# Closing a row-mean kernel: the last store awaited behind the barriers, and the last piece scaled and summed by one accumulating instruction

## The chip, the cores and the metric

The kernel runs on one core of a Trainium2 chip. Its time is the device time of one execution in microseconds; the kernel before takes 162.94 us (median of 4 runs, 162.81 to 163.14). "The span" is what the profile shows: from the first to the last instruction of the program, 161.5 us. The difference is the runtime's own work around the program.

## The reference

```python
batch, seq, dim = 32, 512, 1024
x: float32 [32, 512, 1024]; divisor = 1024.0

def reference(x, divisor):
    return (np.sum(x, axis=-1) / divisor).astype(np.float32)
```

67.1 MB are read and 64 KB written, so the kernel lives from the stream of loads.

## The kernel before

SyncE issues all loads. 16,384 rows lie as 128 partitions of 128 rows; 120 of each go into the output tile `res` in large loads, the last eight into `fin` through ever smaller ones, so that little work is left when the last bytes arrive. The last row of each partition comes in three pieces: `pa` (448 elements, summed by ScalarE), `pb` (256, summed by VectorE) and `pc` (320, with two more columns that take those two sums). `q` collects VectorE's sums; `r` is zero but for one column, where ScalarE puts its share of a row, already scaled. So `fin` is `q` times the scale plus `r`. The end, with cuts:

```python
# ... main loads and sums into res; two small loads into q ...
act_sum(r[:, j : j + 1], row[:, c:], by=scale)                     # ScalarE, 256 elements
nc.vector.reduce_sum(out=q[:, j : j + 1], in_=row[:, :c], axis=AX) # VectorE, 768 elements
# ... loads of pa, pb, pc; res scaled on GpSimd and stored ...
act_sum(pc[:, D - b : D - b + 1], pa)
nc.vector.reduce_sum(out=pc[:, D - b + 1 :], in_=pb, axis=AX)
nc.vector.reduce_sum(out=q[:, L - 1 :], in_=pc, axis=AX)
nc.vector.scalar_tensor_tensor(out=fin, in0=q, scalar=scale, in1=r, op0=MULT, op1=ADD)
tc.keep_in_program_order(nc.sync.dma_start(out=o_last, in_=fin))
```

After this the framework closes the program: SyncE waits for everything that is still under way, the last store included; then come two rounds of a barrier of all engines, between which GpSimd clears the program's semaphores.

Of the kernel before, what the change touches and what calls it, by code (L numbers as in the profile page):

```python
# [1 line left out]

# [4 lines left out]

F32 = mybir.dt.float32
ADD = mybir.AluOpType.add
MULT = mybir.AluOpType.mult  # L10
COPY = mybir.ActivationFunctionType.Copy
AX = mybir.AxisListType.X


def start_loads_at_once(nc):



    sp = mybir.EngineType.SP
    first, body = nc.main_func.blocks[0], nc.main_func.blocks[1]  # L20
    loads = []
    for i in body.instructions:
        if i.engine == sp:
            if type(i).__name__ != "InstDMACopy" or (i.sync_info and i.sync_info.on_wait):
                break
            loads.append(i)
    names = {i.name for i in loads}
    assert names
    body.instructions = [i for i in body.instructions if i.name not in names]
    at = next(  # L30
        k for k, i in enumerate(first.instructions) if i.engine == sp and type(i).__name__ == "InstDrain"
    )
    first.instructions = first.instructions[:at] + loads + first.instructions[at:]


@with_exitstack
def kernel(
    ctx: ExitStack,
    tc: tile.TileContext,
    x: bass.AP,  # L40
    divisor: float,
    out: bass.AP,
):
    nc = tc.nc
    nc.at_finalize(start_loads_at_once)
    xf = x.flatten_outer_dims()
    N, D = xf.shape
    P = nc.NUM_PARTITIONS
    scale = 1.0 / float(divisor)
    J = N // P  # L50
    assert J * P == N


    L = 8
    M = J - L
    x_main = bass.AP(tensor=x.tensor, offset=0, ap=[[M * D, P], [D, M], [1, D]])
    x_last = bass.AP(tensor=x.tensor, offset=P * M * D, ap=[[L * D, P], [D, L], [1, D]])
    o_main = bass.AP(tensor=out.tensor, offset=0, ap=[[M, P], [1, M]])
    o_last = bass.AP(tensor=out.tensor, offset=P * M, ap=[[L, P], [1, L]])


    main = [(14, 0)] * 6 + [(14, 4), (14, 6), (8, 4)]
    last = [(4, 2), (2, 1)]
    assert sum(n for n, _ in main) == M and sum(n for n, _ in last) == L - 2
    bulk = ctx.enter_context(tc.tile_pool(name="bulk", bufs=3))
    one = ctx.enter_context(tc.tile_pool(name="one", bufs=1))
    psum = ctx.enter_context(tc.tile_pool(name="junk", bufs=4, space=bass.MemoryType.PSUM))

    res = one.tile([P, M], F32, name="res")
    fin = one.tile([P, L], F32, name="fin")  # L70
    q = one.tile([P, L], F32, name="q")
    r = one.tile([P, L], F32, name="r")
    nc.gpsimd.memset(r, 0.0)  # L73

    def load(dst, src):
        tc.keep_in_program_order(nc.sync.dma_start(out=dst, in_=src))  # L76

    def act_sum(dst, src, by=1.0):
        n = src.shape[-1]
        junk = psum.tile([P, D], F32, name="junk")  # L80
        nc.scalar.activation(junk[:, :n], src, COPY, scale=by, accum_out=dst)  # L81

    def sums(dst, t, rows, on_act):
        d = rows - on_act
        for i in range(d, rows):
            act_sum(dst[:, i : i + 1], t[:, i, :])
        nc.vector.reduce_sum(out=dst[:, :d], in_=t[:, :d, :], axis=AX)  # L87

    j = 0
    for rows, on_act in main:  # L90
        t = bulk.tile([P, 14, D], F32, name="t")
        load(t[:, :rows, :], x_main[:, j : j + rows, :])
        sums(res[:, j : j + rows], t, rows, on_act)
        j += rows
    j = 0
    for rows, on_act in last:
        t = one.tile([P, rows, D], F32, name=f"t{rows}")
        load(t, x_last[:, j : j + rows, :])
        sums(q[:, j : j + rows], t, rows, on_act)
        j += rows  # L100


    c = 768
    row = one.tile([P, D], F32, name="row")
    load(row, x_last[:, j, :])
    act_sum(r[:, j : j + 1], row[:, c:], by=scale)
    nc.vector.reduce_sum(out=q[:, j : j + 1], in_=row[:, :c], axis=AX)  # L107



    a, b = 448, 704
    pa = one.tile([P, a], F32, name="pa")
    pb = one.tile([P, b - a], F32, name="pb")
    pc = one.tile([P, D - b + 2], F32, name="pc")
    load(pa, x_last[:, L - 1, :a])
    load(pb, x_last[:, L - 1, a:b])
    load(pc[:, : D - b], x_last[:, L - 1, b:])


    nc.gpsimd.tensor_scalar_mul(out=res, in0=res, scalar1=scale)  # L120
    tc.keep_in_program_order(nc.sync.dma_start(out=o_main, in_=res))

    act_sum(pc[:, D - b : D - b + 1], pa)
    nc.vector.reduce_sum(out=pc[:, D - b + 1 :], in_=pb, axis=AX)  # L124
    nc.vector.reduce_sum(out=q[:, L - 1 :], in_=pc, axis=AX)  # L125
    nc.vector.scalar_tensor_tensor(out=fin, in0=q, scalar=scale, in1=r, op0=MULT, op1=ADD)  # L126
    tc.keep_in_program_order(nc.sync.dma_start(out=o_last, in_=fin))


# [1 line left out]
_INS = ['x', 'divisor']  # L131
_OUTS = [((32, 512), 'float32')]

_NUMBERS = {'divisor': 1024.0}


# [26 lines left out]
```

## Time and profile before

| | before |
|---|---|
| time, median of 4 | 162.94 us |
| span of the profiled run (its time 163.29) | 161.5 us |
| last store, issue to landing | 1.4 us |
| landing of the last store to the end of the span | 0.93 us |

The prediction below shows the lines that carry it. One view more, the end of the chain of waits in order of time (start, duration, what). "DVEq" is VectorE's sequencer, which carries out a separate wait instruction; "issue" is time that the profile puts down to nothing:

```profile
157.88 0.42 DVE pc L124
158.30 0.04 DVEq L125
158.33 0.05 issue
158.38 0.50 DVE q L125
158.88 0.03 issue
158.91 0.02 DVEq L126
158.93 0.04 issue
158.98 0.17 DVE fin L126
```

Between any two of the last three instructions about 0.1 us is spent in noticing that the one before is done. The chain ends with the last instruction that computes; the 2.3 us of storing and closing behind it are not in it, and one has to look for them in the waits of SyncE's queue.

### The profile page before, as it was taken

What the parts mean: (1) busy time and instruction counts of PE and PEld (TensorE: products, weight loads), DVE (VectorE), ACT (ScalarE), POOL (GpSimd) and SP (SyncE); (2) the same over time, 40 slices, a digit from 0 to 9 for tenths busy, and PEclk for the clock granted to TensorE, in tenths of its full rate; (3) what the DMA queues carried; (4) which work ended last, traced back from release to release, by engine and by line L of the source; (5) the groups of instructions that cost most, each with busy time, mean ns of one, the idle gap of its engine ahead of it and who ended that gap; (6) DMA issues with size and microseconds to landing.
All of it is one profiled execution on the core that took longest, in us unless ns stands there. A gap on an engine that the chain in (4) does not pass through costs nothing.

```text
span 161.5 us, 138 instructions
## 1 busy us (share of the span) xinstructions
DVE 120.0 (74%) x15; ACT 20.7 (13%) x39; POOL 0.8 (0%) x6
## 2 busy tenths in 40 slices
DVE  0000099968998699959995999599968970697893
ACT  3000000000000000000000000000008100682881
POOL 0000000000000000000000000000000000000100
DMA  9999999999989999999999899999999978999990
GB/s 298 398 440 454 454 454 454 454 440 440 412 355 398 454 454 454 454 454 454 440 440 412 355 398 454 454 454 454 454 454 440 440 327 383 487 414 394 410 384 6
DMA packets 2448, 67.18 MB, mean 416 GB/s; under 512 B 528, under 2 KB 912, under 8 KB 1040
## 3 DMA queue, kind: packets, MB, share of 16 engines
q1 hardware_dynamic: 2448, 67.18, 97.1%
HBM read 67.11 MB, written 0.07 MB: 416 GB/s over the span
## 4 chain that ended last, share of the span: by engine, by line
DMA 67%; DVE 29%; another core or an unknown queue 1%; SPq 1%; issue 0%; DVEq 0%
DMA t<-in_x_dram 45%; DVE res L87 28%; DMA row<-in_x_dram 22%; SPq L76 1%; DVE q L107 1%; DVE q L125 0%; DVE pc L124 0%; DVE fin L126 0%; DVEq L125 0%; DVEq L126 0%
## 5 line engine op out<-in xcount | busy, mean ns | idle before, releaser
L87 DVE TENSOR_REDUCE res<-t 128x14 f32<-128x14336 f32 (+3 forms) x9 | 114.4, 12716 | 38.2 <-DMA t<-in_x_dram 38.2
L81 ACT ACTIVATE junk<-t 128x1024 f32<-128x1024 f32 x17 | 17.2, 1013 | 135.6 <-DMA t<-in_x_dram 135.6
L87 DVE TENSOR_REDUCE q<-t 128x2 f32<-128x2048 f32 (+1 forms) x2 | 3.5, 1752 | 0.7 <-DMA t<-in_x_dram 0.7
L81 ACT ACTIVATION_READ_ACCUMULATOR junk<-t 128x1 f32 x17 | 3.2, 188 | 0.0
L81 ACT ACT_TABLE_LOAD x1 | 1.3, 1283 | 1.7 <-PEq L144 1.7
L120 POOL TENSOR_SCALAR res<-res 128x120 f32<-128x120 f32 x1 | 0.5, 513 | 151.0 <-DVE res L87 151.0
L107 DVE TENSOR_REDUCE q<-row 128x1 f32<-128x768 f32 x1 | 1.0, 953 | 0.1
L125 DVE TENSOR_REDUCE q<-pc 128x1 f32<-128x322 f32 x1 | 0.5, 489 | 0.1
L81 ACT ACTIVATE junk<-pa 128x448 f32<-128x448 f32 x1 | 0.5, 547 | 0.1
L124 DVE TENSOR_REDUCE pc<-pb 128x1 f32<-128x256 f32 x1 | 0.4, 420 | 0.0
L81 ACT ACTIVATE junk<-row 128x256 f32<-128x256 f32 x1 | 0.4, 388 | 0.2 <-DMA row<-in_x_dram 0.2
L126 DVE SCALAR_TENSOR_TENSOR fin<-q,r 128x8 f32<-128x8 f32 x1 | 0.2, 167 | 0.1
L81 ACT ACTIVATION_READ_ACCUMULATOR junk<-row 128x1 f32 x1 | 0.2, 188 | 0.0
L81 ACT ACTIVATION_READ_ACCUMULATOR junk<-pa 128x1 f32 x1 | 0.2, 185 | 0.0
L73 POOL MEMSET r<- 128x8 f32 x1 | 0.1, 105 | 1.3 <-POOLq L144 1.3
L144 POOL MEMSET const-bfloat16-1.0<- 128x1 bf16 x1 | 0.1, 102 | 0.0
L144 POOL MEMSET const-uint8-127<- 128x1 uint8 x1 | 0.1, 102 | 0.0
L144 POOL MEMSET const-float32-0.0<- 128x1 f32 x1 | 0.1, 99 | 0.2 <-issue 0.2
L144 POOL MEMSET const-float32-1.0<- 128x1 f32 x1 | 0.1, 100 | 0.0
## 6 DMA issues: line engine op xcount, KB each, us to landing
t<-in_x_dram SPq DMA_DIRECT2D x8, 7168.0 KB, 35.7
t<-in_x_dram SPq DMA_DIRECT2D x1, 4096.0 KB, 28.5
t<-in_x_dram SPq DMA_DIRECT2D x1, 2048.0 KB, 33.0
t<-in_x_dram SPq DMA_DIRECT2D x1, 1024.0 KB, 35.0
row<-in_x_dram SPq DMA_DIRECT2D x1, 512.0 KB, 35.9
pa<-in_x_dram SPq DMA_DIRECT2D x1, 224.0 KB, 36.0
pc<-in_x_dram SPq DMA_DIRECT2D x1, 160.0 KB, 35.7
pb<-in_x_dram SPq DMA_DIRECT2D x1, 128.0 KB, 35.8
```

The source lines that it names most:

```text
L73: nc.gpsimd.memset(r, 0.0)
L76: tc.keep_in_program_order(nc.sync.dma_start(out=dst, in_=src))
L81: nc.scalar.activation(junk[:, :n], src, COPY, scale=by, accum_out=dst)
L87: nc.vector.reduce_sum(out=dst[:, :d], in_=t[:, :d, :], axis=AX)
L107: nc.vector.reduce_sum(out=q[:, j : j + 1], in_=row[:, :c], axis=AX)
L120: nc.gpsimd.tensor_scalar_mul(out=res, in0=res, scalar1=scale)
L124: nc.vector.reduce_sum(out=pc[:, D - b + 1 :], in_=pb, axis=AX)
L125: nc.vector.reduce_sum(out=q[:, L - 1 :], in_=pc, axis=AX)
L126: nc.vector.scalar_tensor_tensor(out=fin, in0=q, scalar=scale, in1=r, op0=MULT, op1=ADD)
L144: nc = _bacc.Bacc("TRN2", target_bir_lowering=False, num_devices=1)
```

## The change

Its intent is twofold: let the closing barriers run while the last store is in flight, and take one instruction with its wait off VectorE's end. It also reorders the waits of instructions that have several. The first wait of such an instruction stays on it, the others go into a separate instruction ahead, so the wait that ends last should be first. Core of the diff, with cuts; the lines of it that begin with # stand for code left out:

```diff
+def latest_wait_first(nc):
+    def rank(i, w):
+        own = {"DVE": "DVE_", "Activation": "Activation_", "SP": "DVE_", "Pool": "DVE_"}
+        if w.ant_name.startswith("DMAHW") and i.engine != SP:
+            return 0
+        return 1 if w.ant_name.startswith(own.get(...)) else 2
+    # every instruction's waits are sorted by rank
...
+def close_while_storing(nc, landed):
+    # SyncE's closing drain keeps all its waits but those for the last result and its store
...
+    end.instructions = [
+        with_sync(drain, on_wait=tuple(needs.values())),
+        with_sync(store, on_wait=(done,), on_update=(add,)),   # landed += 16
+        *end.instructions[1:-1],                               # the two barrier rounds
+        with_sync(last, on_update=(sub,)),                     # SyncE: landed >= 16, landed -= 16
+    ]
...
+    nc.at_finalize(latest_wait_first)
+    nc.at_finalize(lambda nc: close_while_storing(nc, landed))
...
-    nc.vector.reduce_sum(out=q[:, L - 1 :], in_=pc, axis=AX)
-    nc.vector.scalar_tensor_tensor(out=fin, in0=q, scalar=scale, in1=r, op0=MULT, op1=ADD)
+    nc.vector.scalar_tensor_tensor(
+        out=fin[:, : L - 1], in0=q[:, : L - 1], scalar=scale, in1=r[:, : L - 1], op0=MULT, op1=ADD
+    )
+    scaled = one.tile([P, D - b + 2], F32, name="scaled")
+    nc.vector.tensor_scalar(
+        out=scaled, in0=pc, scalar1=scale, scalar2=0.0, op0=MULT, op1=ADD, accum_out=fin[:, L - 1 :]
+    )
```

More of the change, by code (lines that the diff above doesn't have):

```diff
@@ L1 @@
+import copy
+import dataclasses
 from contextlib import ExitStack
@@ L12 @@
 AX = mybir.AxisListType.X
+SP = mybir.EngineType.SP
 def start_loads_at_once(nc):
-    sp = mybir.EngineType.SP
     first, body = nc.main_func.blocks[0], nc.main_func.blocks[1]
@@ L22, in start_loads_at_once @@
     for i in body.instructions:
-        if i.engine == sp:
+        if i.engine == SP:
             if type(i).__name__ != "InstDMACopy" or (i.sync_info and i.sync_info.on_wait):
@@ L30, in start_loads_at_once, with with_sync @@
     at = next(
-        k for k, i in enumerate(first.instructions) if i.engine == sp and type(i).__name__ == "InstDrain"
+        k for k, i in enumerate(first.instructions) if i.engine == SP and type(i).__name__ == "InstDrain"
     )
     first.instructions = first.instructions[:at] + loads + first.instructions[at:]
+def with_sync(i, on_wait=None, on_update=None):
+    s = i.sync_info
+    return copy.replace(
+        i,
+        sync_info=mybir.SyncInfo(
+            on_wait=s.on_wait if on_wait is None else on_wait,
+            on_update=s.on_update if on_update is None else on_update,
+        ),
+    )
@@ new lines, in latest_wait_first @@
+def latest_wait_first(nc):
[3 more added lines that the diff above has]
+            return 0
+        return 1 if w.ant_name.startswith(own.get(str(i.engine).split(".")[-1], "?")) else 2
+    for block in nc.main_func.blocks[1:2]:
+        block.instructions = [
+            with_sync(i, on_wait=tuple(sorted(i.sync_info.on_wait, key=lambda w: rank(i, w))))
+            if i.sync_info and len(i.sync_info.on_wait) > 1
+            else i
+            for i in block.instructions
+        ]
@@ new lines, in close_while_storing @@
+def close_while_storing(nc, landed):
+    body, end = nc.main_func.blocks[1], nc.main_func.blocks[-1]
+    store = [i for i in body.instructions if i.engine == SP and type(i).__name__ == "InstDMACopy"][-1]
+    (lane,) = store.sync_info.on_update
+    drain = end.instructions[0]
+    assert drain.engine == SP and type(drain).__name__ == "InstDrain"
+    needs = {w.id: w for w in drain.sync_info.on_wait}
+    assert needs[lane.id].wait_value > lane.update_value
+    needs[lane.id] = dataclasses.replace(
+        needs[lane.id], wait_value=needs[lane.id].wait_value - lane.update_value
+    )
+    (done,) = [w for w in store.sync_info.on_wait if w.ant_name.startswith("DVE_")]
+    assert needs[done.id].wait_value == done.wait_value
+    del needs[done.id]
+    own = dict(sync_type="semaphore", id=landed.num, ant_name=landed.name)
+    add = mybir.SyncUpdate(update_mode="sem-add-imm", update_value=16, **own)
+    sub = mybir.SyncUpdate(update_mode="sem-sub-imm", update_value=16, **own)
+    last = nc.sync.wait_ge(landed, 16).ins
+    assert nc.main_func.blocks[-1].instructions[-1].name == last.name
+    body.instructions = [i for i in body.instructions if i.name != store.name]
+    end.instructions = [
[3 more added lines that the diff above has]
+        with_sync(last, on_update=(sub,)),
+    ]
@@ L44 @@
     nc = tc.nc
+    landed = nc.alloc_semaphore("landed")
     nc.at_finalize(start_loads_at_once)
+    nc.at_finalize(latest_wait_first)
+    nc.at_finalize(lambda nc: close_while_storing(nc, landed))
     xf = x.flatten_outer_dims()
@@ L124 @@
     nc.vector.reduce_sum(out=pc[:, D - b + 1 :], in_=pb, axis=AX)
-    nc.vector.reduce_sum(out=q[:, L - 1 :], in_=pc, axis=AX)
-    nc.vector.scalar_tensor_tensor(out=fin, in0=q, scalar=scale, in1=r, op0=MULT, op1=ADD)
+    nc.vector.scalar_tensor_tensor(
+        out=fin[:, : L - 1], in0=q[:, : L - 1], scalar=scale, in1=r[:, : L - 1], op0=MULT, op1=ADD
+    )
+    scaled = one.tile([P, D - b + 2], F32, name="scaled")
+    nc.vector.tensor_scalar(
+        out=scaled, in0=pc, scalar1=scale, scalar2=0.0, op0=MULT, op1=ADD, accum_out=fin[:, L - 1 :]
+    )
     tc.keep_in_program_order(nc.sync.dma_start(out=o_last, in_=fin))
```

## The prediction

> **What bounds the kernel now.** I read the tenths line and the chain of the page first, then the timeline of the last microseconds, then the DMA table, the waits of SyncE's queue, and the instructions of line 158, which is where the closing of the program is put down.
>
> ```profile
> DVE  0000099968998699959995999599968970697893
> ...
> DMA  9999999999989999999999899999999978999990
> ...
> DMA 67%; DVE 29%; another core or an unknown queue 1%; SPq 1%; issue 0%; DVEq 0%
> ```
>
> The DMA line is full from the first slice to the last but one: 67.11 MB of input arrive at 416 GB/s over the span, and for some 158 of the 161.5 us this stream is the limit. (The chain's 29% for VectorE are reductions that a load's buffer had to wait for; other loads were queued meanwhile, and the DMA line stays full through them.) The change touches no load, no buffer and no large reduction, so all that it can win lies after the last bytes have come. This is that stretch, from the timeline (start, duration, instruction):
>
> ```profile
> 156.93 0.95 DVE L107 TENSOR_REDUCE q<-row 128x1 f32<-128x768 f32 x1
> ...
> 157.58 0.55 ACT L81 ACTIVATE junk<-pa 128x448 f32<-128x448 f32 x1
> 157.87 0.42 DVE L124 TENSOR_REDUCE pc<-pb 128x1 f32<-128x256 f32 x1
> 158.07 0.18 ACT L81 ACTIVATION_READ_ACCUMULATOR junk<-pa 128x1 f32 x1
> 158.38 0.49 DVE L125 TENSOR_REDUCE q<-pc 128x1 f32<-128x322 f32 x1
> 158.98 0.17 DVE L126 SCALAR_TENSOR_TENSOR fin<-q,r 128x8 f32<-128x8 f32 x1
> 159.17 0.34 SPq L127 DMA_DIRECT2D out_dram<-fin  x1
> ```
>
> The reader is to see three things. From 156.93 (the landing of `row`) to 159.15 VectorE works without a real rest: four instructions and two gaps, 158.29 to 158.38 and 158.87 to 158.98, together 0.20 us. ScalarE's share is over at 158.25, before VectorE wants it. And after the store's issue nothing is computed, yet the span runs on to 161.5.
>
> ```profile
> SPq L158 <- DMA out_dram<-fin: 0.9, 1, 0.9
> SPq L158 <- PEq L158: 0.6, 2, 0.4
> ```
>
> ```profile
> out_dram<-fin SPq DMA_DIRECT2D x1, 4.0 KB, 1.4
> ```
>
> ```profile
> L158 SPq EVENT_SEMAPHORE  x7: 17/28/912, 159.6 to 161.4; - x7
> L158 POOLq EVENT_SEMAPHORE  x4: 17/17/17, 160.9 to 161.4; - x4
> ...
> L158 SPq DRAIN  x3: 7/7/7, 160.8 to 161.1; - x3
> ```
>
> The store takes 1.4 us from issue to landing: 159.17 + 1.41 = 160.58. SyncE sits in one wait of 912 ns for it. Only then, from 160.6, come its remaining waits, its drain at 160.8, and two rounds of a barrier over all engines until 161.51. So the tail is serial: 2.2 us of VectorE, 0.02 to the issue, 1.41 for the store, 0.93 for closing (161.51 less 160.58).
>
> **What the Trainium skill says.** "DMA: Bandwidth & Descriptors", section "Anatomy of one DMA — SWDGE (gpsimd) path", puts the fixed cost of a DMA mostly to the receipt of the write, heaviest for HBM. That section's two microseconds are for the other issuing path; this trace has 1.41 us for 4 KB, of which 0.34 are the issue, so some 1.06 us are only waiting: time that other work may fill. "Perfetto Trace Analysis", section "Identifying Dependency Chains", says that an instruction with waits on several engines may have EventSemaphore instructions put ahead of it. The trace agrees: each of the two VectorE gaps holds one (55 ns before L125, 21 ns before L126), and ScalarE's reading of `pa`, which landed at 157.50, starts only at 157.58, behind one, where VectorE's L124, with a single wait, starts 0.02 us after its landing. "VectorE: DVE Perf Modes", section "Two Vector instructions with no wait between them", counts an instruction that writes out an accumulator as two, the main one and an accumulator read; no VectorE instruction of this trace does so, but ScalarE's do, and there the read adds 0.12 us (0.185 less an overlap of 0.06). "Runtime: NRT & Kernel Launch", section "The ~15µs preamble/postamble breakdown", has the runtime wait for all engines in a barrier of its own after the kernel. The trace shows semaphore updates on from 161.74, 0.23 us after the last instruction; so a SyncE that ends late holds up that barrier.
>
> **The change part by part.**
>
> (a) The store behind the closing. SyncE now drains everything except the last result, issues the store, and goes straight into the two barrier rounds; a wait for `landed` is its very last instruction. Two chains start at the end of the issue. Barriers: in the kernel before SyncE's entering drain starts at 160.82 and the last engine is through at 161.51, so 0.69 us; with 0.05 us after the issue, 0.74. Store: 1.41 - 0.34 = 1.06 us, plus 0.02 to 0.05 for the wait's own instruction. The store is the longer, so the barriers vanish behind it. With the store issued at the same moment, the end would be 160.58 + 0.03 = 160.61: **0.90 us less span**. The drain's other waits cost nothing: they are passed while SyncE would idle, the last of them (the large store, issued at 153.39, 5.1 us to landing) at 158.5, half a microsecond before the result is ready.
>
> (b) VectorE's end. Removed: the reduction of 322 elements (0.49), the closing scale-and-add behind it (0.17), and both gaps (0.20): 159.15 - 158.29 = 0.86 us from the end of L124. Added: the scale-and-add over seven columns, which needs nothing of L124 and so follows it without a gap: its waits are long satisfied, and instructions with satisfied waits sit back to back here (L124 starts 0.01 before L107 ends). It stays on VectorE's path, since VectorE is the late one: about 0.16. Then the accumulating instruction over 324 elements. The two reductions give the rate: (489 - 420) ns for 66 elements is 1.05 ns each, on a base of 153 ns; 324 elements make 0.49 us, at one element a cycle. Its waits (for `pc`, ScalarE, L124) pass by 158.33, under the scale-and-add. Then the accumulator read: 0.06 to 0.17, the upper end being the smallest VectorE instruction of this trace (167 ns); I take 0.12, as on ScalarE. Sum 0.16 + 0.49 + 0.12 + 0.02 of joints = 0.79 against 0.86: **0.07 us won**. The gaps are what is won, and the read eats half of them.
>
> (c) The order of the waits. ScalarE's starts after a landing come some 0.06 us sooner, GpSimd's scaling of `res` about as much. Neither is on the path: ScalarE is done at 158.25 and is wanted at 158.4. **0.0 us**. SyncE's loads keep their order of waits.
>
> (d) Beyond the span. The other engines now leave the program some 0.35 us before SyncE, so the parts of the runtime's closing barrier that do not need SyncE can go ahead. In the updates after the span the first pass of that barrier has one step of 0.205 us that takes 0.039 in its second pass; about 0.17 us may fall away, if the late engine there is not SyncE. I take half, **0.08 us**.
>
> Sum: 0.90 + 0.07 + 0.08 = 1.05 us. 162.98 - 1.05 = 161.93 us; the span goes from 161.51 to about 160.5.
>
> **The rivals.** *The store becomes the new last wait and the win is smaller.* It does become it; the question is how much it holds. If the wait and the reset of its semaphore at the very end cost more than 0.05, or if the store in flight slows the barrier's semaphore traffic, 0.2 us come back: 162.2. Against it: a satisfied wait takes 17 to 28 ns in the rows above. *The accumulating instruction is slower than the pair it replaces.* If the read cannot follow at once but waits for the main instruction to drain, (b) turns to -0.1: 162.1. For it: one more instruction on an engine that is the path. *It is faster.* The tier table in "VectorE: DVE Perf Modes", section "The perf-mode tier table (the rule you actually need)", gives a plain tensor_scalar in f32 twice the rate, but a reduction only one. At the double rate 0.17 us more are won: 161.76. I choose the single rate[...]. *The end is hidden anyway.* If the time that is measured did not include the closing, nothing of (a) would show and only 0.1 us be won: 162.9. Against it: the profiled run has 163.29 us for a span of 161.5, so more than the span is in it. *The stream itself moves.* Three runs of the kernel before spread over 0.33 us; that noise is a third of the effect.
>
> **Range and chances.** The small uncertainties (0.1 from VectorE, 0.1 from the last wait, 0.1 from the runtime's barrier, 0.15 from the spread of medians) add to about 0.25 in squares; eight in ten is 161.6 to 162.25. Two per cent is 3.26 us, as much as all that follows the last landing (161.51 less 158.25: `pc`, issued at 122.5, lands 35.7 us later), so faster by 2% is out of reach; slower by 2% would need a broken stream. I give each 0.01.
>
> **What will show it.** (a) In the changed profile SyncE's issue of `fin` is followed by barrier entries within 0.1 us, and the last instruction of all is SyncE's wait, ending 1.4 us after the issue; wrong if the barriers end later than the landing. (b) After L124 a gapless scale-and-add of 7 columns, then an instruction near 0.49 us, then an accumulator read; the issue of the store some 0.86 us after the end of L124 or a little sooner (0.88 before). (c) ScalarE's start on `pa` within 0.03 us of its landing, with no effect. (d) The time falls by more than the span. The prediction is wrong if the stream of loads ends at another moment, or if the accumulating pair takes over 0.9 us.

## The result, and the profile after

The changed kernel takes **161.69 us** (median of 4, 161.57 to 161.71), 1.25 us (0.8%) less than before. The ratio is 0.9921, 95% interval 0.9904 to 0.9938. Ratios here and below are the mean time of one kernel's fast runs over that of the other's fast runs of the same rounds, so not quite the ratio of the medians quoted.

The changed kernel's page has the stream as full as before:

```profile
span 160.1 us, 138 instructions
...
DMA  8899999998899999998899999999799999999993
...
DMA 67%; DVE 29%; another core or an unknown queue 1%; SPq 1%; issue 0%; DVEq 0%
```

Its timeline of the end (line numbers have moved by the code added above: L173 is the 768 element reduction, L190 the sum of `pb`):

```profile
156.58 0.95 DVE L173 TENSOR_REDUCE q<-row 128x1 f32<-128x768 f32 x1
...
157.20 0.55 ACT L147 ACTIVATE junk<-pa 128x448 f32<-128x448 f32 x1
157.57 0.17 DVE L191 SCALAR_TENSOR_TENSOR fin<-q,r 128x7 f32<-128x7 f32 x1
157.65 0.41 DVE L190 TENSOR_REDUCE pc<-pb 128x1 f32<-128x256 f32 x1
...
158.18 0.49 DVE L195 TENSOR_SCALAR_CACHE_REDUCE scaled<-pc 128x322 f32<-128x322 f32 x1
158.59 0.08 DVE L195 DVE_READ_ACCUMULATOR scaled<-pc 128x1 f32 x1
158.71 0.34 SPq L198 DMA_DIRECT2D out_dram<-fin  x1
```

The accumulating operation is indeed two instructions, but the read lies almost wholly beside the main one (158.59 to 158.68 against 158.18 to 158.67). The seven columns are scaled *ahead* of the sum of `pb`, not behind it: the framework's scheduler moved them up. And 0.12 us lie idle between the end of that sum (158.06) and the accumulating instruction. The end of the changed kernel's chain of waits says why:

```profile
157.74 0.34 DVE pc L190
158.08 0.04 DVEq L195
158.11 0.07 issue
158.18 0.49 DVE scaled L195
158.67 0.01 DVEq L229
```

The closing, from the changed kernel's waits of SyncE's queue, its DMA table, and its instructions of line 88 (the wait for the landing) and line 229 (the closing):

```profile
SPq L229 <- PEq L229: 0.6, 2, 0.4
...
SPq L88 <- SPq L88: 0.3, 1, 0.3
```

```profile
out_dram<-fin SPq DMA_DIRECT2D x1, 4.0 KB, 1.4
```

```profile
L88 SPq EVENT_SEMAPHORE  x1: 17/17/17, 160.1 to 160.1; - x1
```

```profile
L229 SPq DRAIN  x3: 7/7/132, 158.2 to 159.5; - x3
...
L229 PEldq EVENT_SEMAPHORE  x2: 51/51/51, 159.4 to 159.9; - x2
```

The drain of 132 ns follows the issue of the store. At its start, behind the issue of three loads, the kernel before has one like it (its instructions of line 144):

```profile
L144 SPq DRAIN  x1: 125/125/125, 1.4 to 1.4; - x1
```

The wait of 0.9 us for the store has become one of 0.3 us, behind the barriers: the barrier path has ended by 159.92 (TensorE's instruction of 51 ns that starts at 159.86), the landing wait ends at 160.14.

**Where did 1.25 us come from?** The moment at which the stream ends moves from run to run: in the traced run of the kernel before `row` landed at 156.90, in that of the changed one at 156.56, and the former took 163.29 us, 0.35 above its median. So I measure from fixed points behind the stream. **A** is the time from the end of the 768 element reduction to the issue of the last store, **B** from there to the end of the run (the profiled run's time less the time of the issue). Before: A = 159.17 - 157.88 = 1.29, B = 163.29 - 159.17 = 4.12. Changed: A = 158.705 - 157.535 = 1.17, B = 161.70 - 158.705 = 3.00. Together 5.41 and 4.17, so 1.24 us less, as good as the whole difference of the medians. 0.12 of it is VectorE's end, 1.12 is the closing.

The closing's 1.12 is more than the span shows: from issue to the end of the span 2.34 became 1.44, 0.90 less. The remaining 0.22 us are behind the span. There the runtime runs its own barrier over all engines, and the trace has its semaphore updates (of semaphore 2; they lie in the trace's records, `prof` prints no view of them). Nine updates in a row are one pass; a second pass follows some 0.8 us later. Times in us after the issue of the last store; "end of run" is B, which counts the run's time from the first instruction of the span. In every trace the second pass goes on 0.12 us beyond it, so the last column is true up to a constant, and only its differences are used:

```
            TensorE  SyncE   updates of the runtime's barrier, first pass       end
            ends     ends    1st    2nd    3rd    4th    5th    ...  9th        of run
before      2.338    2.292   2.573  2.607  2.812  2.855  2.878       3.097      4.12
changed     1.210    1.438   1.445  1.479  1.684  1.728  1.751       1.970      3.00
```

The first update comes 0.235 us after TensorE's end in both rows, and everything after it keeps the same distances, to 0.01 us. SyncE's end does not appear: in the changed kernel it lies 0.23 us behind TensorE's, and nothing is later for it. Read this way, the landing of the store no longer sets the time at all.

### The profile page after: what moved, and what is told of

Same layout as the page of the kernel before. It is cut to its first block, busy times and chain, and to the rows that moved or that the text cites. A ratio compares the mean times of both kernels' runs of the same rounds, so it can differ in the third digit from the quotient of the medians.

```text
span 160.1 us, 138 instructions
## 1 busy us (share of the span) xinstructions
DVE 119.9 (75%) x16; ACT 20.7 (13%) x39; POOL 0.8 (1%) x6
## 4 chain that ended last, share of the span: by engine, by line
DMA 67%; DVE 29%; another core or an unknown queue 1%; SPq 1%; issue 0%; DVEq 0%
DMA t<-in_x_dram 45%; DVE res L153 28%; DMA row<-in_x_dram 22%; SPq L142 1%; DVE q L173 1%; DVE scaled L195 0%; DVE pc L190 0%; DVE fin L191 0%; DVEq L195 0%; DVEq L229 0%
## 5 line engine op out<-in xcount | busy, mean ns | idle before, releaser
L173 DVE TENSOR_REDUCE q<-row 128x1 f32<-128x768 f32 x1 | 1.0, 953 | 0.1
L195 DVE TENSOR_SCALAR_CACHE_REDUCE scaled<-pc 128x322 f32<-128x322 f32 x1 | 0.5, 490 | 0.1
L190 DVE TENSOR_REDUCE pc<-pb 128x1 f32<-128x256 f32 x1 | 0.4, 412 | 0.0
```

Of the source, the lines that this page charges most:

```text
L195: nc.vector.tensor_scalar(out=scaled, in0=pc, scalar1=scale, scalar2=0.0, op0=MULT, op1=ADD, accum_out=fin[:, L - 1 :])
```

## The experiments

**Theory T**, formed from that table: TensorE's end of the second barrier round starts the runtime's barrier and sets the time; the landing, for which SyncE alone waits, is hidden. **Rival R**, part (a) of the prediction taken alone: the landing is the longer of the two chains and sets the time. (The whole prediction had 0.98 us for the closing, with the 0.08 of its part (d).) Each run had five timing rounds, of which the record holds five times for e1 to e6 and four for e7 to e10, and the kernel before was run beside it. The table has what came out (the 95% intervals reach about 0.0013 to either side, so single steps of 0.1 us, 0.0006, are read from A and B, not from the times. A and B come from one profiled run each; in the five kernels that close as the changed one does, B is 2.99 to 3.00, so they repeat to about 0.01 us):

| kernel | time, median | before beside it | ratio | A | B | A + B |
|---|---|---|---|---|---|---|
| before | | | | 1.29 | 4.12 | 5.41 |
| changed | 161.69 | 162.94 | 0.9921 | 1.17 | 3.00 | 4.17 |
| e1 closing only | 161.91 | 163.11 | 0.9929 | 1.29 | 2.99 | 4.28 |
| e2 VectorE only | 162.88 | 163.11 | 0.9988 | 1.24 | 4.06 | 5.30 |
| e3 no wait order | 161.75 | 162.97 | 0.9926 | 1.25 | 2.99 | 4.23 |
| e4b landing on TensorE | 161.88 | 163.02 | 0.9929 | 1.17 | 3.14 | 4.31 |
| e5b sixteen waits | 162.00 | 163.02 | 0.9936 | 1.16 | 3.26 | 4.42 |
| e6 own wait first | 161.83 | 163.02 | 0.9927 | 1.09 | 2.99 | 4.08 |
| e7 enter, then issue | 161.73 | 163.02 | 0.9919 | 1.30 | 2.78 | 4.08 |
| e8 seven on GpSimd | 161.60 | 162.97 | 0.9916 | 1.07 | 2.99 | 4.07 |
| e9 = e6 + e7 | 161.42 | 162.97 | 0.9904 | 1.23 | 2.77 | 4.00 |
| e10 = e6 + e7 + e8 | 161.43 | 162.97 | 0.9905 | 1.17 | 2.77 | 3.94 |

### e1: the closing alone

```diff
-    nc.at_finalize(latest_wait_first)
# and VectorE's last two instructions as before
```

> Only the closing is changed (store behind the barriers); VectorE's two closing instructions and the order of the waits are those of the kernel before. Theory T (the time is set by TensorE's end of the last barrier round, 0.235 us after which the runtime's own barrier starts; the store's landing is hidden): from the issue of the last store to TensorE's end 1.21 us instead of 2.34, so time about 1.13 us below before, ratio 0.9931. Rival R (the store's landing, on which SyncE's last wait ends, sets the time): 0.90 us below, ratio 0.9945. Under both the span ends about 1.43 us after the issue and the time less the span falls from 1.78 to about 1.55 under T, stays near 1.78 under R.

The ratio is 0.9929, and B is 2.99, as good as in the changed kernel: 1.13 us less. The time less the span falls from 1.78 to 1.55, as T has it. The trace has the same picture, TensorE's end at 1.206 and the first update at 1.440 after the issue. R's 0.90 falls short of it by what lies behind the span, and its ratio of 0.9945 lies just outside the interval (0.9917 to 0.9942). The prediction's 0.98 for (a) and (d) together would be 0.9940, inside it; what speaks against that sum is B alone, 1.13.

### e2: VectorE's end alone

```diff
-    nc.at_finalize(latest_wait_first)
-    nc.at_finalize(lambda nc: close_while_storing(nc, landed))
```

> Only VectorE's end is changed; closing and order of waits as before. T and R alike: from the end of the 768 element reduction to the issue of the last store 1.17 us (1.29 before), time 0.12 us below before, ratio 0.9993, not to be told from 1 by the times. Time less span stays 1.78. If the two parts are independent, this and the closing alone add to the 1.25 us of the whole change.

A is 1.24, not 1.17: of the 0.12 us only 0.05 are won. I had left out the order of the waits too, and so found that it counts. In this kernel's timeline (L170 is the 768 element reduction, ending at 157.58) the scaling of seven columns comes 0.11 us after that reduction, behind a separate wait instruction; in the changed kernel it comes 0.035 after (157.535 to 157.57).

```profile
156.62 0.95 DVE L170 TENSOR_REDUCE q<-row 128x1 f32<-128x768 f32 x1
...
157.69 0.17 DVE L188 SCALAR_TENSOR_TENSOR fin<-q,r 128x7 f32<-128x7 f32 x1
```

B is 0.06 lower than before as well, because in this build one separate wait fewer stands behind the landing in SyncE's closing; with the new closing there is nothing to win there. In time the interval of e2, 0.9974 to 1.0001, contains 1.

### e3: the changed kernel without the order of the waits

```diff
-    nc.at_finalize(latest_wait_first)
```

> The changed kernel without its reordering of the waits. If the order is worth what the run with VectorE's part alone suggests, the scale-and-add over seven columns starts 0.11 us after the end of the 768 element reduction instead of 0.035, so 1.24 us from that end to the store's issue instead of 1.17, and the time is 0.07 us above the changed kernel's (ratio to before about 0.9928). The prediction on record gave this order 0.0 us: then 1.17 stays.

A is 1.25 and the scaling starts 0.11 us after the reduction, as in e2. B is that of the changed kernel. So the order of the waits is worth 0.08 us of A, on VectorE, and nothing elsewhere. The parts now add up: 1.13 for the closing (e1), 0.04 for VectorE's end without the order (A from 1.29 to 1.25), 0.08 for the order: 1.25. The time (0.9926) agrees, but its interval overlaps the changed kernel's.

### e4b: the landing awaited by TensorE

```diff
-    last = nc.sync.wait_ge(landed, 16).ins
+    last = nc.tensor.wait_ge(landed, 16).ins
```

> The changed kernel with one edit: TensorE, not SyncE, waits for the landing of the last store and takes its semaphore back to zero, as TensorE's last instruction. T (the time is set by TensorE's end; the landing is hidden while it is SyncE that waits for it): TensorE now ends at the landing, about 0.26 to 0.29 us later than in the changed kernel, and so does the runtime's barrier (first update still 0.235 us behind TensorE): about 0.28 us slower than the changed kernel, ratio to before about 0.994. R (the landing sets the end wherever it is waited for): no change, ratio 0.992.

Between the two. TensorE ends 0.27 us later (1.483), the first update comes at 1.762, 0.32 later (0.28 behind TensorE's end, not 0.235), but the step from the second to the third update shrinks from 0.205 to 0.039, and the end of the run is only 0.15 later (B 3.14). So by B it does matter which engine waits for the landing, against R (the times alone, 0.9929 with an interval of 0.9917 to 0.9942, do not tell this run from the changed kernel); but T was too simple: at its third update the runtime's barrier waits for some other engine too, which in the changed kernel is 0.17 us behind. Which one, the records do not tell; that stays open.

### e5b: sixteen further waits on SyncE

```diff
+    more = [nc.sync.wait_ge(landed, 16).ins for _ in range(16)]
...
         *end.instructions[1:-1],
+        *more,
         with_sync(last, on_update=(sub,)),
```

> The changed kernel with sixteen further waits for the landing, satisfied by then, on SyncE (two to an instruction, eight more instructions at about 0.064 us: about 0.5 us more on SyncE's end). R: 0.5 us slower than the changed kernel, ratio to before 0.9955. T: the first update of the runtime's barrier does not move, a later one does, and the cost is 0.5 us less SyncE's slack there, which the records do not give; between 0.2 and 0.45.

SyncE ends 0.49 us later (1.930). The first four updates do not move; the fifth comes at 2.070 instead of 1.751, 0.14 after SyncE's end. The run ends 0.26 us later. So SyncE is met at the fifth update, and it had 0.49 - 0.26 = 0.23 us of slack (0.17 at the fifth update itself, which would follow SyncE's end of 1.438 at 1.578 but comes at 1.751; the rest at the updates behind it). This is against R: in the changed kernel the landing could come about 0.2 us later at no cost. The same records for these three kernels, and for e7 below:

```
            TensorE  SyncE   updates of the runtime's barrier, first pass       end
            ends     ends    1st    2nd    3rd    4th    5th    ...  9th        of run
changed     1.210    1.438   1.445  1.479  1.684  1.728  1.751       1.970      3.00
e4b         1.483    1.164   1.762  1.796  1.834  1.878  1.902       2.120      3.14
e5b         1.210    1.930   1.445  1.479  1.684  1.728  2.070       2.232      3.26
e7          0.735    1.448   0.969  1.004  1.209  1.253  1.589       1.753      2.78
```

### e6: VectorE's own wait first

The idle 0.12 us ahead of the accumulating instruction come from the change's own order: it puts a load's wait first, but here `pc` had landed before (157.91), and it is VectorE's own sum of `pb` (158.06) that ends last.

```diff
         if w.ant_name.startswith("DMAHW") and i.engine != SP:
-            return 0
+            return 1.5 if str(i.engine).endswith("DVE") else 0
```

> The changed kernel with one edit: on VectorE a load's wait is put behind VectorE's own, so that the accumulating instruction itself carries the wait that ends last (the 256 element sum) and the satisfied ones go into the instruction ahead. T and R: the accumulating instruction starts 0.02 us after that sum's end instead of 0.12, so 0.09 us from the end of the 256 element sum to the store's issue, and as much of the time; too little for the times to show surely (ratio 0.9918 against 0.9923).

A falls by 0.08 to 1.09, as expected. The accumulating instruction follows the sum of `pb` (which ends at 158.19) after 0.03 us, in this kernel's timeline:

```profile
157.77 0.41 DVE L190 TENSOR_REDUCE pc<-pb 128x1 f32<-128x256 f32 x1
...
158.22 0.49 DVE L195 TENSOR_SCALAR_CACHE_REDUCE scaled<-pc 128x322 f32<-128x322 f32 x1
158.64 0.08 DVE L195 DVE_READ_ACCUMULATOR scaled<-pc 128x1 f32 x1
```

Alone, the times do not show it (0.9927).

### e7: into the barrier first, then the issue

If the barriers are the bound and the landing has slack, the issue itself (0.34 us of SyncE) should lie beside a barrier round. SyncE must still have passed its wait for the result before it enters, for the semaphores are cleared behind the first round.

```diff
-    del needs[done.id]
+    needs = {done.id: needs.pop(done.id), **needs}     # the drain waits for the result
...
-        with_sync(store, on_wait=(done,), on_update=(add,)),
-        *end.instructions[1:-1],
+        *end.instructions[1:enter],                    # up to SyncE's entry into the first round
+        with_sync(store, on_wait=(), on_update=(add,)),
+        *end.instructions[enter:-1],
```

> The changed kernel with one edit: SyncE waits for the result, enters the first barrier round, and only then issues the last store, so that the issue (0.34 us) lies beside that round. T: TensorE ends about 0.3 to 0.4 us sooner after the result, the store lands 0.05 us later; if SyncE's slack in the runtime's barrier allowed it the time would fall by 0.3, but SyncE then ends 0.6 us behind TensorE, so I expect the landing to become the bound and the gain to be 0.0 to 0.15 us: ratio 0.991 to 0.9925. R: the store lands 0.05 us later, time 0.05 us longer, ratio 0.9926.

TensorE ends 0.48 us sooner after the issue, and B falls by 0.21 to 2.78. A rises by 0.13: the two instructions ahead delay the issue by that much (I had expected 0.05). The sum is 0.08 less than the changed kernel's. Now the fifth update comes 0.14 us behind SyncE's end, as in e5b: here (and in e9 and e10 below) the landing has become the bound, as R had it for the changed kernel.

### e8: the seven columns on GpSimd

```diff
-    nc.vector.scalar_tensor_tensor(out=fin[:, : L - 1], ...)
+    q7 = one.tile([P, L - 1], F32, name="q7")
+    nc.gpsimd.tensor_scalar_mul(out=q7, in0=q[:, : L - 1], scalar1=scale)
+    nc.gpsimd.tensor_tensor(out=fin[:, : L - 1], in0=q7, in1=r[:, : L - 1], op=ADD)
```

> The changed kernel with the scale-and-add over seven columns on GpSimd (a scaling and an addition) instead of VectorE. The 256 element sum then starts 0.08 us sooner, and 1.09 us pass from the end of the 768 element reduction to the store's issue instead of 1.17, if GpSimd is done within that time; time 0.08 us below the changed kernel, ratio to before about 0.9918. If GpSimd's two instructions take over 0.9 us together the store waits for them and it is slower.

A is 1.07. VectorE's sum of `pb` follows the 768 element reduction at once, and GpSimd is done at 158.19, well before the accumulator is read:

```profile
157.59 0.42 DVE L190 TENSOR_REDUCE pc<-pb 128x1 f32<-128x256 f32 x1
157.66 0.25 POOL L192 TENSOR_SCALAR q<-q 128x7 f32<-128x7 f32 x1 [4.71 <-DVE q L173]
...
157.99 0.20 POOL L193 TENSOR_TENSOR fin<-q,r 128x7 f32<-128x7 f32 x1
```

### e9 and e10: the gains together

Edits: those of e6 and e7; those of e6, e7 and e8.

> Own wait first on VectorE together with entering the barrier ahead of the issue. From the end of the 768 element reduction to the issue 1.22 us (1.17 changed, 1.30 with the early entry alone), from the issue to the end of the run 2.78 us (2.995 changed): 0.165 us below the changed kernel, ratio to before about 0.9913. The fifth update of the runtime's barrier should again be 0.14 us behind SyncE's end, as the landing is then the bound.

> Own wait first, early entry and the seven columns on GpSimd. 1.14 us from the end of the 768 element reduction to the issue, 2.78 from the issue to the end of the run: 0.245 us below the changed kernel, ratio to before about 0.9908; the fastest of all if the three gains are independent.

e9 takes **161.42 us** against 162.97, ratio 0.9904 (0.9891 to 0.9918): it is faster than the kernel before. That it also beats the changed kernel rests on A + B, 0.17 us less; the intervals of the two ratios overlap. e10 wins 0.06 more in A (I had expected 0.08), but nothing more in time: 161.43. Its trace shows why A falls short: `pc` lands at 157.85, so the separate wait for it ends at 157.88, with the sum of `pb` and not before it, and the accumulating instruction starts 0.07 us after that sum instead of 0.03. A difference of that size is below what five rounds can tell.

## Why the prediction was right

The time (161.93 foretold, 161.69 measured, range 161.6 to 162.25) and the direction were right, with a forecast win of 1.05 us against 1.25; the mechanism was right only in part. Step by step:

- **What bounds the kernel.** Right: all of the win lies behind the last landing (1.24 of 1.25 us in A + B). By its letter one sign of being wrong came true: in the traced run of the changed kernel the stream ends 0.34 us sooner (`pc` at 157.91, not 158.25). I read it as the noise of the stream: in the runs beside the experiments the span of the kernel before goes from 161.0 to 161.5 us by itself.
- **(a) The store behind the closing, 0.90.** For the span right to the hundredth: 2.338 to 1.438 from the issue to the span's end. The store was also the longer of the two chains. But the step "the store is the longer, so the barriers vanish behind it" is wrong for the time, and so is what it leans on, "a SyncE that ends late holds up that barrier". The runtime's barrier starts from TensorE, so it is the barrier chain that counts, and SyncE's later end has 0.23 us of slack (e5b). The barrier chain's own term was mis-sized as well: 0.74 us after the issue were foretold, 0.87 measured (1.210 less 0.344), because SyncE's drain right behind a DMA's issue takes 132 ns where I had read 7. The trace that I read has such a drain as well, 125 ns at the kernel's start. Both end 0.18 us after the issue ahead of them ends; in e7, where the drain starts 0.13 us after the issue, it takes 49 ns and ends at the same distance.
- **(b) VectorE's end, 0.07.** Without the order of the waits 0.04 to 0.05 (e2, e3), so the size was about right, its terms less so. The accumulating instruction ran at the rate of the reductions, 490 ns as worked out (for 322 elements; the text's 324 is a slip, `pc` has 320 and two). The read adds 6 ns, not 120, since it starts 76 ns before the main instruction ends. In return 0.12 us stand idle ahead of that instruction instead of the 0.02 assumed: the waits do not pass "under the scale-and-add", because the scheduler put that ahead of the sum of `pb`. For the same reason the sign of 0.86 us from that sum to the issue reads 0.64.
- **(c) The order of the waits, 0.0.** Wrong: 0.08 (e3). The step that failed is the choice of where to look. ScalarE's earlier start on `pa` (157.20, 0.02 after its landing) was foretold and is indeed worth nothing; but the same order also works on VectorE, ahead of the seven columns: the separate instruction there now holds ScalarE's wait, satisfied during the reduction before (157.15), where in e3 it holds VectorE's own, which ends last.
- **(d) Behind the span, 0.08.** Right that time would be won there, wrong in size and cause: 0.22. The step of 0.205 us, half of which I counted on, is still there in the changed kernel. What is won is simply that the span's last instruction is now SyncE's, which the runtime's barrier does not need until later.
- **The rivals.** The slower accumulating pair, the double rate and the hidden end all fell; the first, "the store becomes the new last wait", is true of the span only. The stream did move, by about as much as was foretold (0.35 us between the traced run of the kernel before and its median).

The sum: (a) and (d) were foretold as 0.98 and are 1.12; (b) and (c) were foretold as 0.07 and are 0.12. That 0.98 comes so near is in part luck: its (a) rests on a landing that does not set the time, and its (d) on a step that did not change.

## What to carry to other kernels

When a kernel ends with a small store, its landing can be waited for behind everything else, by an engine that the closing needs late (here SyncE; with TensorE it cost 0.15 us): that was 1.1 us here, some nine times the 0.12 us that VectorE's end gave. Which engine ends last in the profile is not yet the one that sets the time; look at what comes after the program, or move a wait from one engine to another and see. Where an instruction has several waits, the one that ends last should sit on the instruction itself, and which that is has to be read from the trace case by case: the general rule of the change was right for ScalarE's loads (a start 0.02 us after the landing, worth nothing here) and wrong for the last sum. A cost read off one place of a trace need not hold in another: the drain of 7 ns became one of 132 ns behind a DMA's issue.

## What the Trainium skill lacked or had wrong

- "Runtime: NRT & Kernel Launch", section "The ~15µs preamble/postamble breakdown", has the closing barrier wait for all engines and, for the one at the start, 44 ns a hop. It calls that barrier a serpentine over five engines, but does not say which engine stands where in it: here the first update follows TensorE's end by 0.235 us, and SyncE is needed only at the fifth, with 0.23 us to spare. A pass that waits for nobody behind TensorE (e4b) takes 0.358 us for its eight hops; in the other runs one hop takes 0.205 us instead of 0.039, since it waits for an engine.
- "VectorE: DVE Perf Modes", section "Two Vector instructions with no wait between them", is right that an accumulator output is a second instruction. No page that I found gives its cost: 82 ns, of which all but 6 lie beside the main instruction.
- The same page's tier table gives tensor_scalar in f32 twice the rate and does not set the accumulating form apart. That form took 490 ns for 322 elements, as long as a reduction of as many (489 ns).
- "Perfetto Trace Analysis", section "Identifying Dependency Chains", tells of the separate wait instructions but not what they cost: a start 0.08 us later ahead of the seven columns (0.11 against 0.035 us), and 0.12 against 0.03 us ahead of the accumulating instruction.
- "DMA: Bandwidth & Descriptors", section "Anatomy of one DMA — SWDGE (gpsimd) path", has about 2 us of fixed cost for that path. For SyncE's path the page has a time to the first byte, but none from issue to landing. For a store of 4 KB from SyncE to HBM the runs show 1.40 to 1.41 us.
- No page that I found says that a drain soon after a DMA's issue takes longer: 125 to 133 ns directly behind it on SyncE, 49 ns when it starts 0.13 us later (e7), against 7 ns with no issue just ahead. In all three it ends 0.18 us after the issue's end.
